# The weight stream's casts, subtractions and sums in one fixed order, from the first MLP slabs on

## The chip, the cores and the metric

The kernel runs on one core of a Trainium2 chip. The metric is the device time of one execution in microseconds; of several runs the median is taken. The trace is of one further execution under the hardware profiler.

## What is computed

One block of a transformer-like encoder on 256 rows of 2048 features in float32: a mixer of four parts (gated linear attention, a Fourier mixer, long convolutions, a short convolution), cross-attention to 256 memory rows, and a gated MLP, each added to the residual, then a final norm. The change touches the MLP and the few products before it:

```
x = x + cross_attention(rms_norm(x, norm_g[l, 1]), mem_n, w_xq[l], w_xkv[l], w_xo[l])
gate, up = jnp.split(h @ w_gate_up, 2, axis=-1)      # h = rms_norm(x, norm_g[l, 2])
x = x + (jax.nn.silu(gate) * up) @ w_down            # 2048 -> 2 x 5632 -> 2048
```

All products keep float32 accuracy. [...]

## The kernel before

**The weight stream.** All weights lie in DRAM in the order of their use, in 252 slabs of 128 x 2048 float32 (1 MB), sixteen blocks of 128 x 128 each. Slabs 0 to 119 belong to the products up to `w_xo`, slabs 120 to 207 to `w_gate_up`, the rest to `w_down`. `GATE_UP` is 128, the ninth slab of the MLP; the eight before it are plain. Class `Stream` (L77) brings them in. `_load` (L104) issues the transfer of a slab from SyncE into one of three buffers `raw` (four in most of the gate/up product). `_half` (L130) makes a plain slab ready in two halves of 128 x 1024: ScalarE casts the half to the high part `wh` (L153) and VectorE subtracts that from the half to get the low part `wl` (L154). The pairs lie in a ring of three to five places that come free when TensorE has used them, and `_fill` (L184) makes as many halves ahead as the ring has places.

**Summed slabs.** In the MLP some pairs of activation rows and weight blocks are multiplied by a scheme with seven products instead of eight, which needs sums of weight blocks. Such a slab (letter S in `GROUPS` and `PASSES`) is made ready by `_sums` (L158) in four parts, each with a cast (L165) and a subtraction (L166). Behind part two VectorE writes the sums that later parts are made from (L176). In `w_down` these are four sums of 128 x 512. In `w_gate_up` part of the summing is done by DMA: SyncE loads a quarter of the slab into a tile of `res` (L113), ScalarE copies it beside itself (L118), and GpSimd issues a transfer that adds the middle half of the slab to it (L120). VectorE then has two sums; the first reads `res`, part three is made from `res`, and part four from the second sum.

**What sets the order.** The program is written with a planner: for each engine it lists the instructions in an order of its own, by priority and by its own estimate of when each is ready. Program order binds it only where data or buffers do, or where `add_manual_dep` ties an instruction behind another on the same engine, without a semaphore. `keep_place` (L335) does that for chosen stretches: each of their instructions is tied behind the one that precedes it in the program on its engine, whatever that is. The copies at L118 are kept in place so; the casts, subtractions and sums of the stream are not. Class `Background` decides where the work between products (norms, splits, fetches of activations) is written in the program. Loads of turned activations go through GpSimd's queue (L591, `load_turned`), their stores too (L586, `store_turned`); splits of activations run on ScalarE and VectorE (helpers at L309 to L325).

**TensorE** takes the stream in program order: in `part` (L457) three matmuls (L459 high by `wh`, L460 high by `wl`, L461 low by `wh`) of 128 x 512 columns each. A half of a plain slab is twelve of them.

In the trace's names, `raw` is a slab as it came, `res` a tile of the summing transfer, `pg` and `pm` are PSUM banks, `hidden` and `features` activations that go through DRAM to be turned, `z` sums of activations.

Of the kernel before, what the change touches and what calls it, by code (L numbers as in the profile page):

```python
# [43 lines left out]
GATE_UP = 1920 // 16 + 8  # L44
# [5 lines left out]
PAIRED = {a + i for a, plan in [(GATE_UP + 8 * j, GROUPS[j % len(GROUPS)]) for j in range(10)] + [(DOWN, PASSES[0]), (DOWN + 22, PASSES[1])]  # L50
          for i, x in enumerate(plan) if x in "Ss"}
# [25 lines left out]
class Stream:  # L77


    def __init__(self, tc, pools, W, bg):  # L80
        self.tc, self.nc, self.W, self.bg = tc, tc.nc, W, bg
        self.rawp, self.wp = pools
        self.order = []
        self.n = self.made = 0
        self.after = []
        self.halves = []
        self.at = self.phase = 0
        self.raw = None
        self.ring = [[self.wp, -1] for _ in range(3)]
        self.raws = [[self.rawp, -1] for _ in range(3)]  # L90
        self.sums = []
        self.places = []
        self.two = []
        self.begun = []
# [34 lines left out]

    def _half(self):  # L130

        nc, n = self.nc, self.made
        if n % 16 == 0 and self.phase == 0:
            self._load(n)
        if n // 16 in PAIRED:
            return self._sums()
        self.made += 8
        o = (n % 16) * P
        r = self.raw[:, o:o + 1024]
        if n >= NBLK - HELD:  # L140
            parts = []
            for a in (0, 512):
                wh, wl = self.places.pop(0)
                nc.scalar.copy(wh, r[:, a:a + 512])
                nc.vector.tensor_tensor(out=wl, in0=r[:, a:a + 512], in1=wh.bitcast(F32), op=ALU.subtract)
                parts.append((wh, wl))
            self.bg.dve(1024)
            self.halves.append(parts)
            return
        wh, wl = self._buffers(n, 1024)  # L150
        edges = [0, 256, 512, 1024] if n == 0 else [0, 512, 1024] if n == 8 else [0, 1024]
        for a, b in zip(edges, edges[1:]):
            nc.scalar.copy(wh[:, a:b], r[:, a:b])  # L153
            nc.vector.tensor_tensor(out=wl[:, a:b], in0=r[:, a:b], in1=wh[:, a:b].bitcast(F32), op=ALU.subtract)  # L154
        self.bg.dve(1024)
        self.halves.append((wh, wl))
# [1799 lines left out]
```

## Time and profile before

| | |
|---|---|
| median of 3 runs | 1442.88 us (1440.34 to 1445.39) |
| the profiled execution | 1443.37 us |
| its span, first to last instruction | 1441.6 us |
| mean granted TensorE clock | 0.997 |
| casts of plain halves, ScalarE L153 | 403, 415.7 us busy |
| subtractions of plain halves, VectorE L154 | 403, 484.4 us busy |
| summed parts: casts of raw L165, subtractions of raw L166 | 165 each, 150.3 and 171.8 us |

The profile gives a page: busy time of each engine, the span in slices, the chain of work that ended last, the costliest groups by line. Other views answer from the same trace: who waited for whom, a timeline of one engine in a window (start, duration, engine, line, operation, out<-in, and in brackets the idle time before it with what ended it), and windows (busy time of TensorE's matmuls and weight loads, VectorE, ScalarE and GpSimd, then granted clock, share of the 16 DMA engines, GB/s). PE is TensorE, DVE VectorE, ACT ScalarE, POOL GpSimd, SP SyncE. [...]

### The profile page before, as it was taken

Reading aid. Unit: us, or ns where it says so; the run is one execution under the profiler, and the core shown is the slowest. Engines: PE = TensorE matmul, PEld = TensorE weight load, DVE = VectorE, ACT = ScalarE, POOL = GpSimd, SP = SyncE. Lnnn points to the kernel's source line nnn. Section 1 sums busy time; section 2 is a strip of 40 time slices with the busy share of each in tenths; the row PEclk is TensorE's granted clock in tenths of the full one; section 3 lists DMA queues with packets and bytes.
Section 4 is the critical chain, followed back from the end, with each engine's and each line's share of the span. In section 5 each row is a group of like instructions: output and inputs, shape, how many; then the busy total and the mean of one; then the engine's idle time right before and its main releaser. Section 6 shows DMA issues by size and latency. Waiting matters only on the chain.

```text
span 1441.6 us, 18611 instructions
## 1 busy us (share of the span) xinstructions
PE 1424.6 (99%) x6574; PEld 1179.6 (82%) x6574; DVE 1162.3 (81%) x1766; ACT 842.0 (58%) x1230; POOL 239.8 (17%) x311
## 2 busy tenths in 40 slices
PE   9999999999999999999999999999999999999997
PEld 7888888888888888888878787888878888888886
DVE  6668868777877667676667988999988888989997
ACT  6566565446655555555556666566666655755655
POOL 0000100013212233530421112122111112100000
PEclk9999999999999999999999999999999999999999
DMA  9886564546667788964887998999898887665564
GB/s 345 295 291 248 204 203 162 175 170 221 202 196 236 234 263 263 273 203 153 285 265 233 280 272 254 295 231 302 244 283 269 256 269 238 216 227 190 188 227 146
DMA packets 71309, 342.74 MB, mean 238 GB/s; under 512 B 10765, under 2 KB 12462, under 8 KB 44080
## 3 DMA queue, kind: packets, MB, share of 16 engines
q1 hardware_dynamic: 52400, 285.31, 56.9%
q0 software_dynamic: 18384, 55.59, 16.6%
q8 instruction: 51, 0.84, 0.2%
q10 hardware_dynamic: 432, 0.66, 0.1%
q14 instruction: 42, 0.34, 0.1%
HBM read 318.97 MB, written 22.54 MB: 237 GB/s over the span
## 4 chain that ended last, share of the span: by engine, by line
PE 87%; DMA 5%; issue 3%; DVE 2%; ACT 1%; POOL 1%; SPq 0%; ACTq 0%; POOLq 0%
PE pg L459 19%; PE pg L461 19%; PE pg L460 19%; PE pm L460 6%; PE pm L461 6%; PE pm L459 6%; PE pg L407 4%; DMA res<-in_W 3%; PE pg L408 2%; DMA raw<-in_W 1%; PE pm L1409 1%; DMA hidden<-g 1%; POOL tmp L591 1%; PE pm L1060 1%; DVE wl L154 1%
## 5 line engine op out<-in xcount | busy, mean ns | idle before, releaser
L154 DVE TENSOR_TENSOR wl<-raw,wh 128x1024 fp32r<-128x1024 f32 (+1 forms) x403 | 484.4, 1213 | 170.6 <-ACT wh L153 167.3
L153 ACT CAST wh<-raw 128x1024 fp32r<-128x1024 f32 (+1 forms) x403 | 415.7, 1042 | 273.9 <-PE pg L461 185.6
L459 PE MATMUL pg<-wh,act 128*128 128x512 f32 (+1 forms) x1161 | 455.3, 392 | 3.0 <-ACT wh L153 3.0
L460 PE MATMUL pg<-wl,act 128*128 128x512 f32 (+1 forms) x1161 | 453.6, 391 | 1.2 <-DVE wl L154 1.2
L461 PE MATMUL pg<-wh,act 128*128 128x512 f32 (+1 forms) x1161 | 453.5, 391 | 0.0
L459 PEld LDWEIGHTS pg<-wh,act 128*128 128x128 f32 x1161 | 218.8, 188 | 50.0 <-ACT wh L153 3.9
L460 PEld LDWEIGHTS pg<-wl,act 128*128 128x128 f32 x1161 | 218.9, 189 | 46.7 <-DVE wl L154 2.3
L461 PEld LDWEIGHTS pg<-wh,act 128*128 128x128 f32 x1161 | 218.8, 188 | 46.5 <-DVE act L309 0.8
L165 ACT CAST wh<-raw 128x1024 fp32r<-128x1024 f32 (+1 forms) x165 | 150.3, 918 | 144.9 <-DVE raw L176 66.8
L166 DVE TENSOR_TENSOR wl<-raw,wh 128x1024 fp32r<-128x1024 f32 (+1 forms) x165 | 171.8, 1060 | 37.0 <-ACT wh L165 36.8
L460 PE MATMUL pm<-wl,act 128*128 128x512 f32 x314 | 122.4, 390 | 0.1
L461 PE MATMUL pm<-wh,act 128*128 128x512 f32 x314 | 122.3, 390 | 0.0
L459 PE MATMUL pm<-wh,act 128*128 128x512 f32 x314 | 122.3, 389 | 0.0
L407 PE MATMUL pg<-act,wh 128*128 128x512 f32 x256 | 90.5, 396 | 0.0
L408 PE MATMUL pg<-act,wl 128*128 128x256 f32 x256 | 71.9, 281 | 0.0
L120 POOL DMA_DIRECT2D res<-in_W x35 | 31.8, 909 | 236.7 <-ACT res L118 236.5
L460 PEld LDWEIGHTS pm<-wl,act 128*128 128x128 f32 x314 | 59.0, 188 | 12.5 <-DVE wl L154 0.4
L461 PEld LDWEIGHTS pm<-wh,act 128*128 128x128 f32 x314 | 59.0, 188 | 12.2
L459 PEld LDWEIGHTS pm<-wh,act 128*128 128x128 f32 x314 | 59.0, 188 | 12.2
L176 DVE TENSOR_TENSOR raw<-raw 128x512 f32<-128x512 f32 x95 | 65.4, 688 | 0.6
L407 PEld LDWEIGHTS pg<-act,wh 128*128 128x128 f32 x256 | 48.2, 188 | 10.4
L165 ACT CAST wh<-res 128x1024 fp32r<-128x1024 f32 x35 | 36.9, 1055 | 32.0 <-DMA res<-in_W 12.2
(376 smaller groups left out, 1895.8 us busy)
## 6 DMA issues: line engine op xcount, KB each, us to landing
raw<-in_W SPq DMA_DIRECT2D x211, 1024.0 KB, 5.4
raw<-in_W SPq DMA_DIRECT2D x35, 768.0 KB, 6.3
res<-in_W POOLq DMA_DIRECT2D x35, 512.0 KB, 9.9
res<-in_W SPq DMA_DIRECT2D x35, 256.0 KB, 5.0
raw<-in_W SPq DMA_DIRECT2D x11, 512.0 KB, 7.6
hidden<-g POOLq DMA_DIRECT2D x22, 256.0 KB, 3.8
tmp<-hidden POOLq DMA_DIRECT2D x44, 128.0 KB, 7.1
features<-tmp POOLq DMA_DIRECT2D x32, 128.0 KB, 4.8
```

Of the source, the lines that this page charges most:

```text
L120: nc.gpsimd.dma_start(t, self.W[SUMS[1][n // 16]][:, 512:1536], accum_op=ALU.add)
L153: nc.scalar.copy(wh[:, a:b], r[:, a:b])
L154: nc.vector.tensor_tensor(out=wl[:, a:b], in0=r[:, a:b], in1=wh[:, a:b].bitcast(F32), op=ALU.subtract)
L165: nc.scalar.copy(wh, src)
L166: nc.vector.tensor_tensor(out=wl, in0=src, in1=wh.bitcast(F32), op=ALU.subtract)
L176: nc.vector.tensor_tensor(out=out, in0=a, in1=b, op=ALU.add)
L407: self.nc.tensor.matmul(p[:, :], wh, slot[:, :], start=start, stop=False)
L408: self.nc.tensor.matmul(p[:, 0:R], wl, slot[:, 0:R], start=False, stop=stop)
L459: self.nc.tensor.matmul(p, hi, wh, start=start, stop=False)
L460: self.nc.tensor.matmul(p, hi, wl, start=False, stop=False)
L461: self.nc.tensor.matmul(p, lo, wh, start=False, stop=stop)
L591: self.nc.gpsimd.dma_start(t.rearrange("p (g t) -> p g t", t=32), src)
```

## The change

A dictionary `last` keeps, for each engine, the name of the stream instruction that was written last. `_half` becomes a frame: it loads when a slab begins, lets `_sums` or `_plain` (the old body of `_half`) write their instructions, and then, from slab 116 on, ties each of these behind the stream instruction before it on the same engine. The loads, the copies at L118, and all work that is not the stream's stay as free as they were; and the ties are for the planner, not for the chip: no semaphore, instruction or buffer is added.

```diff
         self.ring = [[self.wp, -1] for _ in range(3)]
+        self.last = {}
...
     def _half(self):
 
-        nc, n = self.nc, self.made
+        n = self.made
         if n % 16 == 0 and self.phase == 0:
             self._load(n)
-        if n // 16 in PAIRED:
-            return self._sums()
+        ins = self.nc.cur_bb.bb.instructions
+        mark = len(ins)
+        (self._sums if n // 16 in PAIRED else self._plain)()
+        if n // 16 < GATE_UP - 12:
+            return
+        for x in list(ins[mark:]):
+            if x.engine in self.last:
+                self.tc.add_manual_dep(x, self.last[x.engine], mybir.DependencyInfo(
+                    mybir.DependencyClass.NoSync, mybir.DependencyReason.DATA), reason="order")
+            self.last[x.engine] = x.name
+
+    def _plain(self):
+
+        nc, n = self.nc, self.made
         self.made += 8
```

## The prediction

> **What bounds the kernel now.** I read the page first: busy shares, then the 40 slices.
>
> ```profile
> span 1441.6 us, 18611 instructions
> PE 1424.6 (99%) x6574; PEld 1179.6 (82%) x6574; DVE 1162.3 (81%) x1766; ACT 842.0 (58%) x1230; POOL 239.8 (17%) x311
> ```
>
> TensorE is busy 99% of the span, so an edit that removes no matmul can win at most TensorE's idle time and any time at a low clock. The next view is therefore who TensorE waited for, from 720 to 1200 us, a stretch that holds the end of attention and the whole gate/up product.
>
> ```profile
> PE pm L460 <- DVE wl L166: 2.8, 4, 0.8
> PE pg L459 <- ACT wh L153: 1.9, 1, 1.9
> PE pg L460 <- DVE wl L154: 0.9, 1, 0.9
> PE pm L459 <- ACT wh L165: 0.5, 2, 0.3
> ```
>
> The columns are microseconds in total, times, and the longest. That is 2.8 us at plain slabs (L153, L154) and 3.3 us at summed slabs (L165, L166). All of it is waiting for casts and subtractions, exactly the instructions that the change orders.
>
> **The plain wait stands at one place**, where the MLP begins. I read it in the timelines of ScalarE, VectorE and TensorE, cut into narrow windows so that single instructions show.
>
> ```profile
> 727.75 1.05 ACT L153 CAST wh<-raw 128x1024 fp32r<-128x1024 f32 x1 [1.67 <-PE pg L461]
> 735.70 2.94 ACT L153 CAST wh<-raw 128x1024 fp32r<-128x1024 f32 x3 [6.91 <-DMA raw<-in_W]
> 736.65 1.04 ACT L153 CAST wh<-raw 128x1024 fp32r<-128x1024 f32 x1
> 736.78 1.23 DVE L154 TENSOR_TENSOR wl<-raw,wh 128x1024 fp32r<-128x1024 f32 x1 [6.73 <-ACT wh L153]
> 737.92 1.22 DVE L154 TENSOR_TENSOR wl<-raw,wh 128x1024 fp32r<-128x1024 f32 x1
> 735.48 0.39 PE L461 MATMUL pg<-wh,act 128*128 128x512 f32 x1
> 737.75 0.50 PE L459 MATMUL pg<-wh,act 128*128 128x512 f32 x1 [1.88 <-ACT wh L153]
> 739.20 0.50 PE L460 MATMUL pg<-wl,act 128*128 128x512 f32 x1 [0.95 <-DVE wl L154]
> ```
>
> Three casts start when a transfer lands. TensorE, out of work since 735.87, begins at the end of the second cast (736.65 + 1.04 = 737.69) and its second matmul at the end of the second subtraction (737.92 + 1.22 = 739.14). So the first cast, the one that waited 6.91 us, was not the one TensorE needed: a later slab's cast stands ahead of an earlier one's. The chain that ended last names the transfer, and the DMA columns of a windows view bound the other one.
>
> ```profile
> 724.70 10.98 DMA raw<-in_W
> 740.61 0.43 PE pg L459
> 743.60 0.43 PE pg L460
> 744.02 0.23 PE pg L461
> 722.50 0.33 SPq L126 DMA_DIRECT2D raw<-in_W  x1
> 722.50:727.00 4.50, 4.50 (x21) 3.72 (x21) 2.74 (x4) 2.37 (x3) 3.48 (x4) 1.00 0.84 202
> 727.00:731.50 4.50, 4.50 (x22) 3.72 (x21) 1.56 (x2) 1.05 (x1) 0.03 (x1) 1.00 1.02 320
> 740.00:745.00 5.00, 5.00 (x16) 3.97 (x15) 5.00 (x12) 2.38 (x5) 2.48 (x4) 0.66 0.73 244
> ```
>
> Two slabs of 1 MB were asked for, at 722.50 and 724.70, and the second landed at 735.68. In the windows the last two columns are DMA share and GB/s: 0.91 MB moved up to 727.0 and 1.44 MB in the next 4.5 us. I estimate that the first slab was in by 729 to 731. After the stall the granted clock (the column before) falls to 0.66 in that stretch: eight matmuls, from 740.61 to 743.60, come 0.43 us apart instead of 0.23, which is 8 x 0.20 = 1.6 us more. The entry to the MLP thus costs 1.9 + 0.9 + 1.6 = 4.4 us.
>
> **The summed waits** stand at four places and look alike. The first, on VectorE, ScalarE and TensorE, and behind it the rows of TensorE (and one of VectorE) that place the other three:
>
> ```profile
> 808.94 0.69 DVE L176 TENSOR_TENSOR raw<-res,raw 128x512 f32<-128x512 f32 x1 [0.90 <-DMA res<-in_W]
> 810.03 1.23 DVE L166 TENSOR_TENSOR wl<-res,wh 128x1024 fp32r<-128x1024 f32 x1 [0.40 <-ACT wh L165]
> 811.17 0.69 DVE L176 TENSOR_TENSOR raw<-raw 128x512 f32<-128x512 f32 x1
> 811.78 1.22 DVE L154 TENSOR_TENSOR wl<-raw,wh 128x1024 fp32r<-128x1024 f32 x1
> 812.98 1.22 DVE L166 TENSOR_TENSOR wl<-raw,wh 128x1024 fp32r<-128x1024 f32 x1
> 811.89 1.05 ACT L165 CAST wh<-raw 128x1024 fp32r<-128x1024 f32 x1 [0.95 <-DVE raw L176]
> 811.92 0.39 PE L460 MATMUL pm<-wl,z 128*128 128x512 f32 x1
> 813.05 0.44 PE L459 MATMUL pm<-wh,z 128*128 128x512 f32 x1
> 814.25 0.50 PE L460 MATMUL pm<-wl,z 128*128 128x512 f32 x1 [0.76 <-DVE wl L166]
> 894.43 1.23 DVE L166 TENSOR_TENSOR wl<-res,wh 128x1024 fp32r<-128x1024 f32 x1 [0.41 <-ACT wh L165]
> 895.71 0.50 PE L460 MATMUL pm<-wl,z 128*128 128x512 f32 x1
> 898.65 0.50 PE L460 MATMUL pm<-wl,z 128*128 128x512 f32 x1 [0.76 <-DVE wl L166]
> 982.17 0.50 PE L460 MATMUL pm<-wl,z 128*128 128x512 f32 x1 [0.74 <-DVE wl L166]
> 1066.50 0.50 PE L460 MATMUL pm<-wl,z 128*128 128x512 f32 x1 [0.52 <-DVE wl L166]
> ```
>
> A summed slab gives four parts. After the summing transfer lands, program order is: sum, sum, subtraction of part three (from res), subtraction of part four (from raw), then the next plain slab's subtraction. The list has it otherwise: the second sum stands behind part three, and the plain L154 passes part four, for which TensorE stops.
>
> **The change part by part.** It adds and removes no instruction, transfer or buffer; from slab 116 on it only fixes, within ScalarE and within VectorE, which stream instruction follows which. It adds no wait between engines. What costs is what now stands behind what.
>
> *Entry.* The earlier slab's cast comes first. With data by 731, cast (1.05) and subtraction (1.22) are done by 733.4, 2.3 us before TensorE runs dry at 735.87. If the landing were as late as the second slab's 735.68, the lower bound of the gain applies: the cast still goes first, and one cast interval (736.65 - 735.70 = 0.95) is won; less than nothing it cannot be, since TensorE takes the halves in slab order anyway. At best all 4.4 us are won. I take 4.4, the nearer to my estimate. The second slab's cast stays at 735.70; TensorE reaches it two halves of about 2.7 us (12 matmuls at 0.23) later, at 741, so it is covered by 3 us. The next load is issued when a subtraction frees its buffer, so it goes out earlier.
>
> *Summed slabs.* From the rows above, start to start, a sum takes 0.60 and a subtraction 1.14. Sums at 808.94 and 809.54 (ending 810.23), part three's subtraction at 810.14, part four's cast from 810.25 to 811.30, its subtraction from 811.33 to 812.55. It was done at 814.20 and is needed at 813.28 (0.23 behind 813.05). So 1.65 us are won where 0.76 were lost, and 0.73 remain in hand. Part three comes 0.11 later, at 811.37, and is needed at 811.92. The plain subtraction slips from 811.78 to 812.5; its first matmul comes six matmuls, 1.4 us, after part four's, at 814.7 to 815, so 1 us of cover remains. At the second place part three was itself just in time (894.43 + 1.23 = 895.66, used at 895.71), so its 0.1 us is paid there; I book the same once more for the other two. Sum: 3.3 - 0.2 = 3.1 us.
>
> *The rest.* In the down product the four sums now come behind part two's short subtraction (0.69 us). TensorE waits for none of these lines there (the four rows of waits are all that it has behind the kernel's first microseconds), so nothing is booked. If it were gone, it would cost up to 0.7 us at each of six summed slabs, 4 us. Untied work (evacuations, activation splits, the copies at L118) can still be placed anywhere between; a shift of the planner's making is bounded by about the same 3 us either way, and I take none.
>
> [...]
>
> **Sum.** 4.4 + 3.1 = 7.5 us. The profiled execution took 1443.4 us (span 1441.6 and 1.8 around it), 0.5 above the median 1442.88 of the three runs. 1443.4 - 7.5 = **1435.9**, which I give as 1436.0. A measurement of this kernel can tell about 0.3% (4.3 us) from no change.
>
> **Rivals.**
>
> *The landing decides, not the list.* At all four summed places the chain goes through a transfer of about 11 us (next rows). If TensorE arrives 4.4 us earlier at a transfer that cannot start earlier, the four gains are eaten again. For it: DMA share is 1.03 from 805 to 810. Against: its start hangs on TensorE's end of the previous group. Time: 1443.4 - 4.4 = 1439.0.
>
> *The entry stays.* If the first slab's cast waits for a buffer or lands late, only the summed slabs win: 1443.4 - 3.1 - 0.9 = 1439.4. If the lists stay in effect as they are, 1443.
>
> *Slower: the summing transfer goes out later.* GpSimd's list is laid out by the same planner and is not tied.
>
> ```profile
> 881.52 11.72 DMA res<-in_W
> 805.00:810.00 5.00, 5.00 (x24) 4.14 (x23) 3.37 (x4) 2.73 (x4) 0.00 (x0) 1.00 1.03 353
> L591 POOL DMA_DIRECT2D tmp<-hidden x26 | 24.4, 999 | 25.1 <-issue 13.3 <-DMA hidden<-g 7.2 <-DVE z L309 4.5
> POOL res L120 <- ACT res L118: 236.5, 24, 18.6
> ```
>
> The summing transfer (L120) is issued behind its copy (L118) and shares GpSimd's list with the loads of hidden features (L591, 1.0 us each, four at a time). Should it fall behind four more, it lands 4.0 us later. The new order gives back 1.65, so each of the four places loses 2.35 more than now, 9.4 together; gaps of 3 us also halve the clock as at the entry, 4 x 1.6 = 6.4. Less the entry's 4.4 that is + 11.4: 1455. It decides from a slip of 1.65 + 4.4/4 = 2.75 us. For it: GpSimd mostly waits for the copy (236.5 us), so the copy's place sets the start. Against: the copy stands behind part four's cast, which comes 1.6 us earlier. [...]
>
> **How the numbers follow.** Forecast 0.52; landing decides 0.14; entry stays or nothing happens 0.14; slower 0.20. The forecast lies below 1438.5 nearly always, the second and third cases about one time in four: faster by over 0.3% 0.58, within 0.22, slower 0.20. The range runs from 1433.0 (all 7.7 us of waits and clock gone, and the low end of the runs, 2.5 below the median) to 1446.0 (both middle cases with the high end of the runs and some of the slower one).
>
> **What would show it.** TensorE's waits for L153 and L154 near 737 gone, with no stretch at a clock of 0.66; casts there in slab order, the first starting near 730; sum directly behind sum at each summed slab, part four ahead of the plain L154; the waits for L166 down from 2.8 to some tenths. It would be wrong if TensorE waited for L165 or L166 at new places with a DMA of res as the releaser, or if L120 stood behind more L591 than now.

## The result and the profile after

Line numbers of the kernel after are those of before + 13 (L153 is L166, L165 is L178, L176 is L189, L459 is L472), and + 1 in `_load` (L120 is L121).

| | before | after |
|---|---|---|
| median, same chip | 1445.24 us (1440.34 to 1447.85, 12 runs) | 1436.79 us (1432.77 to 1440.07, 12 runs) |
| ratio, 95% interval | 1 | 0.9945 [0.9931, 0.9959] |
| profiled execution, its span | 1443.37, 1441.6 us | 1437.34, 1435.6 us |

The time fell by 0.55%, some 8 us between runs and 6.0 us between the two profiled executions; 1436.0 was forecast. The page after and TensorE's waits from 720 to 1200 us:

```profile
span 1435.6 us, 18619 instructions
PE 1421.5 (99%) x6574; PEld 1178.7 (82%) x6574; DVE 1164.5 (81%) x1766; ACT 841.8 (59%) x1230; POOL 239.6 (17%) x311
```

```profile
PE pm L473 <- DVE wl L179: 2.0, 3, 1.0
PE pm L472 <- ACT wh L178: 1.8, 1, 1.8
```

The plain waits (2.8 us) are gone. The summed ones are 3.8 us where they were 3.3: the change won at the entry, and at the summed places nothing is left of the 3.1 us that were booked.

**The entry.** ScalarE, VectorE and TensorE where the MLP begins, from the timelines of after:

```profile
729.35 1.05 ACT L166 CAST wh<-raw 128x1024 fp32r<-128x1024 f32 x1 [1.67 <-PE pg L474]
732.07 1.05 ACT L166 CAST wh<-raw 128x1024 fp32r<-128x1024 f32 x1 [1.67 <-PE pg L474]
734.70 2.00 ACT L166 CAST wh<-raw 128x1024 fp32r<-128x1024 f32 x2 [1.17 <-DMA raw<-in_W]
733.15 1.23 DVE L167 TENSOR_TENSOR wl<-raw,wh 128x1024 fp32r<-128x1024 f32 x1 [1.50 <-ACT wh L166]
735.95 0.39 PE L472 MATMUL pg<-wh,act 128*128 128x512 f32 x1
```

The two casts that stood behind the 6.91 us wait now run at 729.35 and 732.07, as soon as TensorE frees a place. The cast that waits for a transfer comes behind them, at 734.70, and TensorE takes 12 matmuls per half without a gap (in the records each is 0.39 us long and starts 0.23 us behind the one before). The clock stays up there: 1.00 over 735 to 745 us, where it was 0.83.

**The first summed place**, VectorE, ScalarE and TensorE, answering to the rows of 808 to 814 us:

```profile
801.67 0.69 DVE L189 TENSOR_TENSOR raw<-res,raw 128x512 f32<-128x512 f32 x1
802.40 0.69 DVE L189 TENSOR_TENSOR raw<-raw 128x512 f32<-128x512 f32 x1
803.01 1.22 DVE L179 TENSOR_TENSOR wl<-res,wh 128x1024 fp32r<-128x1024 f32 x1
804.28 1.23 DVE L179 TENSOR_TENSOR wl<-raw,wh 128x1024 fp32r<-128x1024 f32 x1
805.43 2.47 DVE L167 TENSOR_TENSOR wl<-raw,wh 128x1024 fp32r<-128x1024 f32 x2
803.20 1.05 ACT L178 CAST wh<-raw 128x1024 fp32r<-128x1024 f32 x1 [0.46 <-DVE raw L189]
805.53 0.39 PE L473 MATMUL pm<-wl,z 128*128 128x512 f32 x1
```

This is the order that was foretold: sum, sum, part three, part four, and only then the plain subtraction. Part four is done 3.84 us after the first sum began (801.67 to 804.28 + 1.23) where it took 5.26 (808.94 to 814.20). It is needed at 805.53, so it comes with nothing in hand.

**The third summed place** is where the loss sits. GpSimd, SyncE, ScalarE, VectorE and TensorE in after:

```profile
954.36 3.56 POOL L604 DMA_DIRECT2D tmp<-hidden  x4 [4.37 <-issue]
957.88 0.99 POOL L121 DMA_DIRECT2D res<-in_W  x1
955.95 2.93 SPq L127 DMA_DIRECT2D raw<-in_W  x2
965.60 0.62 ACT L178 CAST wh<-raw 128x512 fp32r<-128x512 f32 x1 [0.32 <-PE pg L474]
971.65 1.05 ACT L178 CAST wh<-res 128x1024 fp32r<-128x1024 f32 x1 [5.43 <-DMA res<-in_W]
971.63 0.69 DVE L189 TENSOR_TENSOR raw<-res,raw 128x512 f32<-128x512 f32 x1 [4.50 <-issue]
972.75 0.50 PE L472 MATMUL pm<-wh,z 128*128 128x512 f32 x1 [1.81 <-ACT wh L178]
974.24 0.80 PE L473 MATMUL pm<-wl,z 128*128 128x512 f32 x1 [0.99 <-DVE wl L179]
```

The summing transfer goes out at 957.88 and lands at 971.55, 13.67 us later; ScalarE idles 5.43 us for it, then TensorE 1.81 and 0.99. The windows view shows the price behind it (the columns after the engines are clock, DMA share, GB/s):

```profile
974.20:977.50 3.30, 3.26 (x8) 2.59 (x9) 3.25 (x3) 3.30 (x6) 0.10 (x1) 0.50 0.57 137
977.60:981.00 3.40, 3.40 (x16) 2.79 (x16) 3.32 (x5) 2.34 (x3) 0.68 (x1) 1.00 0.97 298
```

Eight matmuls in 3.3 us at a clock of 0.50, sixteen in the 3.4 us behind. The half-clock stretch of the entry came back here. In before TensorE's only wait at this place was the 0.74 us at 982.17, for part four. The transfer there, from the timelines of GpSimd and ScalarE in before:

```profile
961.51 3.56 POOL L591 DMA_DIRECT2D tmp<-hidden  x4 [2.78 <-issue]
965.50 0.93 POOL L120 DMA_DIRECT2D res<-in_W  x1 [0.43 <-ACT res L118]
976.86 1.05 ACT L165 CAST wh<-res 128x1024 fp32r<-128x1024 f32 x1 [1.75 <-DMA res<-in_W]
```

Out at 965.50, landed at 976.77: 11.27 us. GpSimd's list has the same order in both kernels (four loads, then the summing transfer).

### The profile page after: what moved, and what is told of

It reads as the page before. It is cut to its first block, busy times and chain, and to the rows that moved or that the text cites. A ratio compares the mean times of both kernels' runs of the same rounds, so it can differ in the third digit from the quotient of the medians.

```text
span 1435.6 us, 18619 instructions
## 1 busy us (share of the span) xinstructions
PE 1421.5 (99%) x6574; PEld 1178.7 (82%) x6574; DVE 1164.5 (81%) x1766; ACT 841.8 (59%) x1230; POOL 239.6 (17%) x311
## 4 chain that ended last, share of the span: by engine, by line
PE 86%; issue 5%; DMA 4%; DVE 3%; ACT 1%; POOL 1%; SPq 0%; ACTq 0%; POOLq 0%
PE pg L474 19%; PE pg L472 19%; PE pg L473 19%; PE pm L473 6%; PE pm L474 6%; PE pm L472 6%; PE pg L420 4%; DMA res<-in_W 2%; PE pg L421 2%; PE pm L1422 1%; DMA hidden<-g 1%; PE pm L1073 1%; DVE wl L179 1%; DVE raw L189 1%; DVE wl L167 1%
## 5 line engine op out<-in xcount | busy, mean ns | idle before, releaser
L166 ACT CAST wh<-raw 128x1024 fp32r<-128x1024 f32 (+1 forms) x403 | 415.4, 1042 | 269.9 <-PE pg L474 182.8
L472 PE MATMUL pg<-wh,act 128*128 128x512 f32 (+1 forms) x1161 | 453.6, 391 | 0.6 <-ACT wh L166 0.6
L472 PEld LDWEIGHTS pg<-wh,act 128*128 128x128 f32 x1161 | 218.1, 188 | 46.9 <-issue 1.5
L178 ACT CAST wh<-raw 128x1024 fp32r<-128x1024 f32 (+1 forms) x165 | 150.6, 919 | 132.8 <-DVE raw L189 47.1
L472 PE MATMUL pm<-wh,act 128*128 128x512 f32 x314 | 122.2, 389 | 0.0
L121 POOL DMA_DIRECT2D res<-in_W x35 | 31.8, 907 | 230.9 <-ACT res L119 230.9
L472 PEld LDWEIGHTS pm<-wh,act 128*128 128x128 f32 x314 | 59.0, 188 | 12.1
L189 DVE TENSOR_TENSOR raw<-raw 128x512 f32<-128x512 f32 x95 | 65.3, 688 | 1.5
L178 ACT CAST wh<-res 128x1024 fp32r<-128x1024 f32 x35 | 36.9, 1054 | 45.3 <-DMA res<-in_W 18.9
L420 PEld LDWEIGHTS pg<-act,wh 128*128 128x128 f32 x256 | 48.1, 188 | 10.5
```

Of the source, the lines that this page charges most:

```text
L121: nc.gpsimd.dma_start(t, self.W[SUMS[1][n // 16]][:, 512:1536], accum_op=ALU.add)
L178: nc.scalar.copy(wh, src)
L189: nc.vector.tensor_tensor(out=out, in0=a, in1=b, op=ALU.add)
L420: self.nc.tensor.matmul(p[:, :], wh, slot[:, :], start=start, stop=False)
L472: self.nc.tensor.matmul(p, hi, wh, start=start, stop=False)
```

## The experiments

For a table by place I took the same stream matmuls in each trace (the start of an L459 matmul, counted in program order) at both ends of five stretches: in before 735.03 to 759.77 (entry) and 789.01 to 829.80, 869.92 to 914.88, 959.76 to 999.76 and 1039.88 to 1085.25 (the summed places). Lengths in us; the time is the median of all runs that were compared.

| kernel | entry | place 1 | 2 | 3 | 4 | four | span | time | ratio |
|---|---|---|---|---|---|---|---|---|---|
| before | 24.74 | 40.79 | 44.96 | 40.00 | 45.37 | 171.12 | 1441.6 | 1443.3 to 1445.2 | 1 |
| after | 19.72 | 39.44 | 43.75 | 43.68 | 44.19 | 171.06 | 1435.6 | 1436.79 | 0.9945 |
| after again | 19.72 | 39.44 | 44.20 | 42.83 | 44.27 | 170.74 | 1435.5 | 1436.14 | 0.9944 |
| ties on 116 to 127 | 19.72 | 39.85 | 44.68 | 41.92 | 44.86 | 171.31 | 1436.7 | 1437.23 | 0.9953 |
| ties from 128 on | 25.43 | 41.71 | 43.04 | 43.11 | 45.17 | 173.03 | 1444.0 | 1444.05 | 0.9995 |
| wy lent later, no tie | 19.99 | 40.21 | 44.53 | 41.05 | 45.67 | 171.46 | 1436.6 | 1437.82 | 0.9959 |
| ties on ScalarE | 19.72 | 40.22 | 45.73 | 40.45 | 45.54 | 171.94 | 1437.5 | 1439.75 | 0.9965 |
| ties on VectorE | 22.64 | 39.44 | 44.23 | 40.14 | 44.14 | 167.95 | 1435.2 | 1440.26 | 0.9982 |
| both, then VectorE | 19.72 | 46.05 | 43.47 | 40.55 | 44.97 | 175.04 | 1439.1 | 1436.64 | 0.9953 |
| four loads halved | 19.72 | 39.44 | 44.11 | 40.20 | 44.80 | 168.55 | 1433.1 | 1434.85 | 0.9938 |
| no tie, lead 3 | 23.02 | 40.04 | 43.26 | 39.18 | 43.85 | 166.33 | 1433.8 | 1437.11 | 0.9955 |
| ties on 116 to 127, lead 3 | 19.72 | 39.85 | 43.25 | 39.18 | 43.85 | 166.13 | 1430.3 | 1432.12 | 0.9922 |
| all ties, lead 3 | 19.72 | 39.44 | 42.84 | 38.76 | 43.52 | 164.56 | 1428.9 | 1431.10 | 0.9909 |

The spans hold 0 to 1.4 us more of difference in the first 300 us, which comes and goes between executions of unchanged code there (294.7 us in before, 293.3 to 294.9 in the others).

My theory after the result: the entry gave 5 us by order alone; at the summed places the order gave some tenths to 1.4 us each, but what binds there is the landing of the summing transfer, and the new order let it land later. The rival: the ties of the paired slabs win their 3 us, and the third place is an accident of one profile.

**The kernel after, once more.**

> The changed kernel once more, to see what of its trace repeats. Theory (the list's order decides the entry and the summed slabs, and the landing of the summing transfer decides what is left): the stretch from the last product of attention into the MLP again takes about 19.7 us where it took 24.7 before, and no 6.9 us wait of a plain cast; the one long wait of the first trace (1.81 and 0.99 us at 973 to 974 us, behind a transfer that took 13.7 us to land) may be absent or stand at another of the four places, since it hangs on a landing. Rival (the tied list makes the third place worse, whatever the landing): the same wait of 2.8 us stands at the third place again. Time about 8 us below before under both.

1436.14 us (1433.38 to 1439.77), ratio 0.9944 [0.9926, 0.9962]. The third place is long again (42.83) with a landing of 13.93 us and a half-clock stretch, so it is no accident of one execution, though not every execution has it (below, at the halved loads).

**The two halves of the change.** In `_half`, the ties on slabs 116 to 127 alone, and those from 128 on alone:

```diff
-        if n // 16 < GATE_UP - 12:
+        if not GATE_UP - 12 <= n // 16 < GATE_UP:
             return
```

> Ties only for the slabs 116 to 127, the plain ones at the entry of the MLP. Theory: the entry's 24.7 us fall to 19.7 and the waits for L179 (part four) stay at about 0.76 us each at four places: about 5 us faster than before, 0.997. Rival (the entry is free, the whole gain comes from the summed slabs): no change against before. Rival (the landing eats what the entry wins): the waits at the four summed places grow by what the entry gave, and the time stays within 2 us of before.

1437.23 us (1435.63 to 1438.99), ratio 0.9953 [0.9937, 0.9968].

```diff
-        if n // 16 < GATE_UP - 12:
+        if n // 16 < GATE_UP:
             return
```

> Ties only from slab 128 on, where summed slabs begin; the entry's casts stay in the planner's order. Theory: the entry takes 24.7 us as before, with the wait of 6.9 us and the half clock; the waits at the summed places shrink from 3.3 us in all to well under 1 us unless a transfer lands late: about 3 us faster than before, 0.998. Rival (landing decides at the summed places): no change against before, and the waits stay, now with a transfer of res as what ends them.

1444.05 us (1441.01 to 1445.74; the profiled execution is the slowest of these twelve), ratio 0.9995 [0.9985, 1.0005]. Nearly the whole effect comes with the ties on the twelve slabs at the entry; the ties on the paired slabs, which were to bring 3.1 us, bring nothing that can be measured. Their third place is 43.11 us long without any change at the entry, so it doesn't take an earlier TensorE to make the transfer late. But the paired ties aren't needed for it either: with the ties at the entry alone the place is 41.92 us long, against 40.00 in before.

**One slab more of lead for the summing transfer**, with all ties:

```diff
-AHEAD = (-2, -2)
+AHEAD = (-3, -3)
```

> The changed kernel with the summing transfer begun three slabs ahead in place of two; nothing else. If the landing decides what is left at the four places, TensorE has no wait for L178 or L179 in the gate/up product any more, and the time falls by 2 to 5 us against the changed kernel (to 0.991 to 0.993 of before). If the list's order decides, the waits stay where they are, and the time is that of the changed kernel (0.9945). If the transfers only crowd each other more, slower than the changed kernel.

1431.10 us (1430.55 to 1431.40), ratio 0.9909 [0.9892, 0.9927]. TensorE has no wait left from 720 to 1200 us. GpSimd and ScalarE at the third place:

```profile
946.46 1.57 POOL L599 DMA_DIRECT2D hidden<-g  x2 [9.17 <-DVE g L597]
948.02 0.96 POOL L121 DMA_DIRECT2D res<-in_W  x1
952.33 3.56 POOL L604 DMA_DIRECT2D tmp<-hidden  x4 [3.36 <-issue]
965.22 1.06 ACT L178 CAST wh<-res 128x1024 fp32r<-128x1024 f32 x1
```

The transfer now stands ahead of the four loads, right behind the stores. It goes out 17.2 us ahead of its cast and lands 9.3 us later, so nobody waits. The same edit without any tie, and with the ties at the entry alone:

> The kernel before, without any tie, with every slab requested one slab earlier (AHEAD -3 in place of -2). Theory A (the summed places wait for the landing of the summing transfer, whatever the order of the lists): the four idle gaps of TensorE at the summed places (2.8 us in four, in the profile of before) and most of what the segments there are longer than in the kernel with ties and lead 3 go away: the four places 3 to 5 us shorter than in before, while the entry stays at about 24.7 us, since nothing undoes its inverted casts: some 1439 to 1441, a ratio of 0.996 to 0.998. Theory B (the interleaved sums themselves hold the stream on VectorE): the four gaps stay at about 0.7 us each, and the time stays within 1 us of before (ratio 0.9993 to 1.0007).

1437.11 us (1435.61 to 1438.46), ratio 0.9955 [0.9940, 0.9970]. TensorE's waits from 720 to 1200 us are the entry's alone:

```profile
PE pg L459 <- ACT wh L153: 1.8, 1, 1.8
PE pg L460 <- DVE wl L154: 0.9, 1, 0.9
```

The four waits for L166 of before are gone although VectorE's list still has the second sum behind part three. This is the plainest answer to my prediction: those 2.8 us were the price of a landing, and order could only make up for it. The four places are 4.8 us shorter than before.

> Ties only on the twelve slabs ahead of the paired ones, and lead 3; the sums and casts of the paired slabs are left as in the kernel before. Theory A (with the landing early, the ties of the paired slabs are worth nothing): the same time as with all ties and lead 3, 1430 to 1432, ratio 0.990 to 0.992 and no idle gap of TensorE over 0.3 us at the summed places. Theory B (the ties of the paired slabs take the sums out of the way and are worth the 3.1 us that the prediction gave them once the landing doesn't hide it): 1433.5 to 1435, ratio 0.993 to 0.995, with gaps of about 0.7 us left at the four places.

1432.12 us (1431.49 to 1433.27), ratio 0.9922 [0.9908, 0.9936]. No wait of TensorE is left here either. Against all ties with the same lead the four places take 1.57 us more, some 0.4 each: matmul intervals of 0.30 and 0.34 in place of 0.23 at the low parts. That is what the order of the paired slabs is worth where the landing is early. In the times the two can't be told apart.

**The entry by other means.** The kernel before, without a tie, with the ring's place `wy` lent one step later:

```diff
-                self.st.lend(self.wy)
...
+                self.st.lend(self.wy)
                 self.st.lend(self.wz)
```

> The kernel before, without any tie, with the place of wy lent to the ring one step later (where wz is lent). Theory A (the entry stalls because a slab with a fresh place of the ring is cast ahead of the slab in front of it, so that its landing holds back casts whose data lies there): with the place lent later the stall at 735 to 745 us is gone without a tie: entry 20 to 21.5 us in place of 24.7, ratio 0.996 to 0.998, unless the inversion only moves to a slab behind, where it would show as a gap of its own. Theory B (the entry stalls because the loads come too late at that place, however the casts are ordered): a wait of about the same length (2 to 3 us, with the half clock behind it) stays at the entry, ratio 0.999 to 1.002, or above 1 since the ring has one place fewer for a while.

1437.82 us (1435.46 to 1439.25), ratio 0.9959 [0.9944, 0.9974]. The entry takes 19.99 us. ScalarE there:

```profile
730.23 1.05 ACT L153 CAST wh<-raw 128x1024 fp32r<-128x1024 f32 x1 [2.12 <-DMA raw<-in_W]
732.51 1.05 ACT L153 CAST wh<-raw 128x1024 fp32r<-128x1024 f32 x1 [1.23 <-PE pg L461]
735.49 1.05 ACT L153 CAST wh<-raw 128x1024 fp32r<-128x1024 f32 x1 [1.52 <-DMA raw<-in_W]
```

So the first slab lands at 730.1 (inside the 729 to 731 that I had estimated), and the second near 735.4. The stall came from the planner's using a place that had just been lent: a cast of the second slab had somewhere to go at once, while the first slab's two casts had to wait for TensorE to free theirs, and it went ahead.

**One engine's list alone.** The loop over the new instructions skips the other engine.

```diff
         for x in list(ins[mark:]):
+            if x.engine != mybir.EngineType.Activation:
+                continue
```

> The ties on ScalarE's list alone; VectorE's sums stay interleaved as before. Theory A (the entry is ScalarE's order; the summed places are gained on VectorE's list and lost where a weight load of the next slab goes ahead of the summing transfer): entry 19.7 to 20.5 us, the four summed places together within 1 us of before's 171.1 us, no gain there: 1436 to 1438.5, ratio 0.994 to 0.9965. Theory B (both lists are needed at the entry): entry over 22 us, ratio 0.997 to 0.999.

1439.75 us (11 runs, 1438.04 to 1440.86 and one of 3705.78), ratio 0.9965 [0.9952, 0.9978]: the entry's full gain and none at the summed places, as its first theory had it.

```diff
         for x in list(ins[mark:]):
+            if x.engine != mybir.EngineType.DVE:
+                continue
```

> The ties on VectorE's list alone; ScalarE's casts are left as in the kernel before. Theory A (the entry's 5 us come from ScalarE's two casts that stand behind the cast of the later slab; VectorE only follows): the entry stays at 24 to 25 us and the time at 1443 to 1445 (ratio 0.999 to 1.001), as with the ties on the paired slabs alone. Theory B (VectorE's list is what the entry waits for): entry 20 to 21 us and a time of 1436 to 1438.5, ratio 0.994 to 0.996.

1440.26 us (1436.96 to 1446.43), ratio 0.9982 [0.9969, 0.9995]. The entry's stall is still ScalarE's:

```profile
734.11 2.94 ACT L168 CAST wh<-raw 128x1024 fp32r<-128x1024 f32 x3 [6.62 <-DMA raw<-in_W]
736.15 0.49 PE L474 MATMUL pg<-wh,act 128*128 128x512 f32 x1 [1.59 <-ACT wh L168]
737.41 0.50 PE L475 MATMUL pg<-wl,act 128*128 128x512 f32 x1 [0.77 <-DVE wl L169]
```

The expected 1443 to 1445 was missed for two reasons: in the profiled execution no half-clock stretch followed, and the four places are 3.2 us shorter than before. That execution, 1436.96 us, is the fastest of the twelve and 3.3 us below their median, so its trace shows more than a typical run won. Of the kernels with a lead of 2 that leave nothing out, this alone shows the 3.1 us of my prediction.

**Both lists at the entry, VectorE's alone behind it**, to add the two gains:

```diff
         for x in list(ins[mark:]):
+            if n // 16 >= GATE_UP and x.engine != mybir.EngineType.DVE:
+                continue
```

> Both lists tied on the twelve slabs ahead of the paired ones, VectorE's list alone tied from there on. Theory A (with VectorE alone tied the casts of ScalarE keep the weight loads from running ahead of the summing transfer at the third place, so the 3.2 us that the ties on VectorE alone gained at the four places come on top of the entry's 5.0): span some 1432.5 to 1433.5, time 1433.5 to 1435.5, ratio 0.9925 to 0.9945, third place near 40.1 us with no half clock. Theory B (the third place is a matter of the time at which the places are reached, not of ScalarE's ties): third place 42 to 44 us with a gap of 0.9 us or more ahead of the high-part matmul, and 1436 to 1437.5 as with all ties.

1436.64 us (1433.87 to 1444.61), ratio 0.9953 [0.9937, 0.9970]. The sum did not come out. In the profiled execution the third place was as expected (40.55), but the first took 46.05 us: there the summing transfer went out 10.5 us into the stretch, landed 13.1 us later, and TensorE idled 2.18 and 0.99 us. In the windows view of this kernel the low clock lasts twice as long as in after:

```profile
808.00:811.30 3.30, 2.59 (x6) 2.11 (x7) 3.23 (x4) 3.30 (x5) 0.00 (x0) 0.50 0.47 113
811.40:814.70 3.30, 3.30 (x9) 2.59 (x8) 3.08 (x4) 2.95 (x4) 0.88 (x1) 0.50 0.84 254
815.00:818.00 3.00, 3.00 (x14) 2.44 (x14) 3.00 (x6) 0.87 (x1) 0.00 (x0) 1.00 1.01 295
```

So a late landing isn't bound to ScalarE's ties, which this kernel lacks behind the entry. This execution took 1440.83 us, 4.2 above the median, so most of the others can't have lost as much there; why the transfer was late, no run shows.

**Less on the DMA engines.** With all ties, four loads bring half a slab each; the other half of the slab is left out of the product. Each was meant to be the load directly ahead of the summing transfer at one of the four places:

```diff
+HALVED = {GATE_UP + i for i in (14, 30, 46, 62)}
...
+        if n // 16 in HALVED:
+            nc.sync.dma_start(self.raw[:, 0:1024], self.W[n // 16][:, 0:1024])
+            return
...
-        o = (n % 16) * P
+        o = 0 if n // 16 in HALVED else (n % 16) * P
```

> All ties, lead 2, but in each of the four places the load of the slab that stands directly ahead of the summing transfer brings 0.5 MB in place of 1 MB: its second half of columns is left out and the first half is used twice, so this part of the product is left out. Theory A (the summing transfer lands late because it shares the DMA engines with the weight load that went ahead of it): landing 10 to 11.5 us in place of 12.5 to 13.7 at the second to the fourth place, the idle time ahead of the high-part matmul at the third place gone or under 0.4 us, no half clock there, third place 39.5 to 41 us in place of 43.7: 1432 to 1434, ratio 0.9915 to 0.994. Theory B (the summing transfer takes 12 to 14 us by itself at these places, or because of GpSimd's own four loads ahead of it): landing stays over 12 us, third place 42 us or more, 1436 to 1437.5.

1434.85 us (1432.54 to 1440.36), ratio 0.9938 [0.9914, 0.9961]. The edit missed its aim. The halved loads (L128) go out at 828.39, 911.96, 996.05 and 1079.56 us, each 2.9 to 6.0 us behind the end of a place; at the third place a load of 1 MB still goes out beside the summing transfer. SyncE there and at the third halved load:

```profile
956.39 2.93 SPq L131 DMA_DIRECT2D raw<-in_W  x2
996.05 0.33 SPq L128 DMA_DIRECT2D raw<-in_W  x1
```

So for the third place this run tests neither theory; it is in effect one more execution of all ties. The place took 40.20 us without a half clock, as the first theory had it, but the landing still took 13.65 us. GpSimd there:

```profile
947.94 1.56 POOL L603 DMA_DIRECT2D hidden<-g  x2 [5.42 <-DVE g L601]
952.86 3.56 POOL L608 DMA_DIRECT2D tmp<-hidden  x4 [2.40 <-issue]
956.38 0.99 POOL L122 DMA_DIRECT2D res<-in_W  x1
```

The transfer went out earlier than in after. The chain on GpSimd's queue, read from such rows and the landings in each trace of a kernel with a lead of 2, third place, in us from the start of the stretch; the last column is the length of the place less the landing (* where the clock fell):

| kernel | VectorE's list | store of hidden lands in | summing transfer out at | lands in | landed at | place 3 | less the landing |
|---|---|---|---|---|---|---|---|
| before | free | 4.01 | 5.74 | 11.27 | 17.01 | 40.00 | 22.99 |
| ties on ScalarE | free | 3.95 | 5.43 | 12.18 | 17.62 | 40.45 | 22.83 |
| wy lent later, no tie | free | 4.23 | 5.74 | 12.32 | 18.06 | 41.05 | 22.99 |
| ties on VectorE | tied | 4.37 | 5.64 | 12.82 | 18.46 | 40.14 | 21.68 |
| four loads halved | tied | 3.61 | 4.87 | 13.65 | 18.52 | 40.20 | 21.68 |
| both, then VectorE | tied | 4.75 | 6.01 | 12.88 | 18.89 | 40.55 | 21.66 |
| ties on 116 to 127 | free | 5.14 | 6.40 | 12.53 | 18.93 | 41.92 | 22.99 |
| after again | tied | 4.36 | 5.62 | 13.93 | 19.56 | 42.83 | 23.27 * |
| ties from 128 on | tied | 4.88 | 6.15 | 13.70 | 19.84 | 43.11 | 23.27 * |
| after | tied | 5.57 | 6.82 | 13.67 | 20.49 | 43.68 | 23.19 * |

The second store leaves GpSimd at the same point of the stretch in all of them (2.8 us ahead of its start). When it has landed, the four loads go out, and the summing transfer goes out 4.0 to 4.5 us after that landing.

The last column has three values: 22.8 to 23.0 us with VectorE's list free, 21.7 with it tied, and 1.6 more than that where the clock fell. So in these traces each microsecond of landing costs one, and at the same landing the tied list saves 1.3 us. The other places agree: length less landing is 21.5 to 21.7 us free and 20.3 tied at the second, 24.2 and 23.0 at the fourth. What is left with the list tied is a gap of 0.99 us, as at 974.24 in after, ahead of the matmul that takes part three's low part, whose subtraction now stands behind both sums.

What makes the landing late is shown in part. The DMA engines are busy there in both kernels (0.97 to 1.03 from 953 to 969 us in after, 0.96 to 1.06 from 960 to 980 us in before). In the six kernels with VectorE's list tied a weight load goes out 4.89 us into the stretch (955.95 in after, 1.9 us ahead of the summing transfer), in the others at 5.90 or 6.39 (966.15 in before, 0.65 us behind it); and the summing transfer takes 12.8 to 13.9 us in those six, 11.3 to 12.5 in the others. That is about what the tied list saves, taken back. The halved loads bear this out where they did go: the four summing transfers right behind them land in 7.00 to 8.41 us, and the same ones in 9.69 to 10.86 us in the two executions of after (8.06 to 11.14 in the other seven kernels with this lead). How the DMA engines divide their time between two transfers no run shows. The rest of the delay is the moment of issue. It follows the landing of the store, which took 5.57 and 4.36 us in two executions of the same kernel, and what moves that stays open.

**The best version once more**, all ties and a lead of three:

> All ties and a lead of three slabs once more, beside the other kernels of this call: 1430 to 1432, ratio 0.990 to 0.9925, entry 19.7 us, no gap of TensorE over 0.3 us after 700 us; the four places 164.6 us together, 1.6 us less than without the ties of the paired slabs at the same lead.

1431.84 us (1431.51 to 1432.43), ratio 0.9913 [0.9888, 0.9938], again without a gap of TensorE over 0.4 us behind 700 us. It is some 5 us faster than the change alone and its runs lie within 0.9 us, where those of the change spread over 6 to 7.

## Why the total was right and one of its terms was not

*What bounds the kernel* held: TensorE, 99% busy, and only its idle time and its clock could be won.

*Entry, 4.4 us*: right in mechanism, a little small in size. The stretch became 5.02 us shorter, since the two stalls cost more than the idle column says: from 735.48 to 737.75, 739.20 and 739.53 in before, TensorE's starts lie 0.16, 0.27 and 0.10 us further apart than the 0.23 of a full pipe and the idle 1.88 and 0.95 us account for. The first slab's landing at 730 (seen without ties), the cover of the second slab, and the clock that stays up all came as worked out. Ties on ScalarE alone give all of it, ties on VectorE alone don't: it was ScalarE's list.

*Summed slabs, 3.1 us*: **this is the step that failed.** The order and the shorter chain on VectorE came (3.84 us from the first sum to part four done, where I had 3.61 and before had 5.26), and places 1, 2 and 4 are 1.35, 1.21 and 1.18 us shorter. The order is even worth more than I booked: 1.2 to 1.3 us at each of the places 2 to 4 at the same landing, and the 1.35 of the first, some 5 us together. But I had held the landing of the summing transfer fixed and booked only what stood behind it in VectorE's list, so that "part three comes 0.11 later" was all that it could lose. The landing moved. At place 3, which I had counted like the others, the transfer lands 3.5 us later in the stretch and the place is 3.68 us longer, where 0.74 was to be won: 3.5 for the landing and 1.6 for the clock, less 1.3 for the order. The four together changed by -0.06 us, and the ties from 128 on alone by nothing that can be measured (0.9995 [0.9985, 1.0005]).

The two runs with a lead of three show why the reading was too short. VectorE's wrong order was the last thing ahead of TensorE's wait, so the view named L166; but with the landing 8 to 11 us earlier the same order costs no wait at all. The list and the landing were two lengths of one chain, and I shortened the one that I could see.

*Rivals.* "The landing decides, not the list" is what came out at the summed places, with 1439.0 us for the whole: the landing took back what the list won. Its own reason, that TensorE arrives earlier, is not needed, since it shows without the entry's gain too. "The entry stays" and "nothing happens" are out. The slower rival did not come: GpSimd's list has the same order, and the transfer's issue slipped by 1.1 us into the stretch, not by the 2.75 from which it would decide. But its sign to watch for, TensorE waiting for L165 with a transfer of `res` behind it, is exactly what the third place shows, and its warning that such a gap halves the clock came true once (1.6 us).

*The sum* still came near, 1435.9 against 1437.3 for the profiled execution, and in part by luck: 4.4 was 5.0, 3.1 was 0.1, and about 1 us came from the first 300 us of the trace, where no instruction changed its place. Between the medians the change is worth some 8 us, 2 more than between the two traces; what these are made of, no trace shows.

## What to carry to other kernels

When an engine's list looks inverted behind a wait, ask first when the data came: if a transfer's landing is in the same chain, move the transfer (here one slab of lead, 4.8 us at four places without any tie) and only then the list (1.6 us more). A cast that waits for a transfer must not stand ahead of one whose data is there (in before one at the entry waited 6.91 us and held two others); fresh buffers invite a planner to do just that, and either a tie or a later loan of the buffer cures it. And when an order frees buffers earlier, look at which transfers go out earlier, and at what shares the DMA engines with them (behind half a slab the summing transfer landed in 7.00 to 8.41 us, behind a whole one, in the two executions of after, in 9.69 to 10.86).

## What the runs showed of the hardware

**Where the clock fell in these traces.** The trace's record of the clock has stretches at 0.50 of 3.413 us, or of 6.827 us once (both lists tied at the entry, VectorE's alone behind it), besides the one in which every trace ends. Within one execution they begin whole multiples of 3.413 us apart: in before at 740.48 and, at the end, 1436.80 (204.0 times 3.413), in after at 974.17 and 1431.56 (134.0), with the ties from 128 on at 740.42 and 982.77 (71.0). I added up TensorE's idle time (by the modelled ends of its matmuls) in windows of that length on that grid, over the fourteen traces. A clock that was up stayed up behind every window with 1.52 us or less (1.44, 1.47, 1.49, 1.52 are the largest) and fell behind every one with 1.63 us or more (1.63, 1.66, 1.74, 2.00, 2.43, 2.72; the 1.63 is before's from 737.06 to 740.48, the 2.72 after's from 970.76 to 974.17). The stretch of 6.827 us is a case of its own: its first window, already at half clock, held 0.73 us of idle time, and the clock did not come back behind it. So here stalls of much the same length cost 1.6 us more or nothing more, by where they lay on the grid: 1.78 + 0.95 us at the entry without ties and with a lead of 3 fell into two windows and cost nothing more, while 0.87 + 0.99 us at the third place of the second run of after fell into one, all but 0.2 us, and did. Kernels with such a stall also spread more (1436.96 to 1446.43 us with ties on VectorE, 1431.51 to 1432.43 without a stall); whether the clock is the reason, no run shows.

**The summing transfer**, which adds 0.5 MB to its target, took 6.0 to 13.7 us to land in after, and 11.2 to 13.7 us at the four places, where it stood in GpSimd's queue behind four small loads; the view by line of after:

```profile
L121 POOL DMA_DIRECT2D res<-in_W x35: 850/882/996, 757.5 to 1163.5; - x35
DMA to landing us min/median/max: 6.0/9.7/13.7
```
